# dt's 16 columns in a quarter of v: one step fewer in the mixer of a hybrid decoder layer, and five stretches of written order

## The chip, the cores and the metric

The kernel runs on one core of one Trainium2 chip. The metric is the time of one execution in microseconds (us), the median of the runs. Engines are named as the profile names them: PE is TensorE (matmuls; PEld its weight loads), DVE is VectorE, ACT is ScalarE, POOL is GpSimd, SP is SyncE, whose queue issues most of the loads.

## What is computed

One decoder layer over 512 tokens of width 1024: a SwiGLU FFN, a mixer, a second FFN, a gated embedding, and a last norm. The mixer is the part that the change is about:

```python
n = rmsnorm(h, mix_norm[i])
proj = n @ w_in[i]
u, v, z, xbc, dt_raw = jnp.split(proj, IN_SPLITS, axis=-1)
ya = chunked_spatial_gating(jax.nn.gelu(u, approximate=False), jax.nn.gelu(v, approximate=False), ...)
ya = rmsnorm(ya, gm_out_norm[i])
yb = mamba2_mixer(z, xbc, dt_raw, conv_w[i], conv_b[i], dt_bias[i], a_log[i], d_skip[i], ssm_norm[i])
h = h + jnp.concatenate([ya, yb], axis=-1) @ w_out[i]
```

Of `w_in`'s 4624 columns, u, v and z have 1024 each, xbc has 1536 (x 1024, B 256, C 256) and dt has 16, one for each head of the SSM. Inside `mamba2_mixer`, xbc goes through a causal convolution of width 4 and silu, and dt through a softplus with a bias; dt then scales x and, cumulatively summed, makes the decays. v is used after gelu and a layer norm over its 1024 columns.

## The kernel before

All matmuls keep near-float32 precision by splitting each operand into a high and a low part: `whi` is a copy of a weight tile rounded by ACT (the **cast**), `wlo` is what is left, taken on DVE (the **low**). A product is then three matmuls (`passes`, L219): hi x hi, hi x lo, lo x hi.

The work is a list of **steps**. A step has a load (SP's queue, 512 KB, 128x1024), a cast, a low, a product on PE, and work after the product. There are 2 steps of embedding, 98 of the first FFN, 37 of the mixer, 16 of the output projection, and then the second FFN. For the mixer the steps are, in order (L1177):

```python
"B0 B1 dt C0 C1 x0 v0 x1 x2 x3 v1 x4 x5 v2 x6 x7 z0 v3 z1 v4 z2 v5 z3 v6 z4 v7 z5 u0 z6 u1 z7 "
"u2 u3 u4 u5 u6 u7"
```

B, C, x, z and u are projections onto 128 columns for all 512 tokens: 24 matmuls of 512 columns. v is needed with tokens on the partitions, so a v step takes two of the eight 128-row pieces of the contraction and adds them into four PSUM banks, one for each 128 tokens, 512 columns of v wide: 24 matmuls of 512 columns. v0 to v3 make v's first half, v4 to v7 the second; gelu reads the four banks after v3 and after v7 (`v_kept`).

dt has a step of its own (`dt_step`, L1143): its 16 columns, twice, fill a 128-column tile so that one product of 16 matmuls gives the high and the low half. dt comes out with heads on the partitions; `dt_kept` copies it (L1262), four transposes on PE put tokens on the partitions (L1267), `dt_sum` adds the halves, applies the norm's row scale `rtok` and the bias, and `softplus` follows. `sums_of_adt`, `decays_of_sums`, `sums_by_row` and `rows_to_dram` make the decays from it.

B and C pass through `conv`: `begin` copies a product out of its bank, scaled by the norm's row scale (L1228), `end` does three operations of DVE for the taps (L1238), and a silu on ACT follows. The norm of the mixer's input itself is made while B0 and B1 run: sums of squares on PE (L288), a chain of small operations on DVE, a broadcast on PE (L325). The input x is split by ACT (L210) and DVE (L211), and B0 takes its last two pieces of x behind its other six.

Each engine runs its instructions in the order in which the program issues them. That order is set by `run`: for each step it issues product, cast (two steps ahead), low, the work after the step before, and so on, and each of these is a task with a name (load, product, cast, split for the low, after, rest, post, and the number of the step). The table `ENTRY` is an order written out by hand for the first stretch of the program: names of tasks, with a count of pieces where only a part of it is issued. What `ENTRY` does not name is issued in `run`'s own order behind it. Tiles come from rings of buffers: `whi`, `wlo` and `raw` have three each, so the cast of a step waits for the product of the third step before.

In the FFNs, a group makes gate and up products into banks named mm and a (L725), DVE and ACT turn them into g, which is split into `ghi` (ACT, L894) and `glo` (DVE, L896), and the down product (L235) goes into banks named sm, which DVE adds to h (L930). `whix` and `wlox` are the halves of the down weights.

Of the kernel before, what the change touches and what calls it, by code (L numbers as in the profile page):

```python
# [60 lines left out]
after13  # L61
# [16 lines left out]
HEADS = 16  # L78
HD = 64
# [20 lines left out]
def layer_kernel(ctx: ExitStack, tc: tile.TileContext, a: dict, out: bass.AP):  # L100
# [254 lines left out]
    class RowNorm(Norm):  # L355
# [52 lines left out]
    def run(steps, opened, order):  # L408
# [64 lines left out]
    class Parts:  # L473


        def __init__(self, tag="raw"):
            self.tag, self.n = tag, 1024

        def load(self, src, n=1024):
            self.n = n  # L480
# [5 lines left out]
            nc.sync.dma_start(self.raw[:, :n], src)  # L486
# [22 lines left out]
        def cast(self, x=""):  # L509
            self.take(x)  # L510
            nc.scalar.copy(self.hi[:, : self.n], self.raw[:, : self.n])  # L511

        def low(self):
            n = self.n
            nc.vector.tensor_tensor(  # L515
                self.lo[:, :n], self.raw[:, :n], self.hi[:, :n].bitcast(F32), ALU.subtract
            )
# [577 lines left out]
    w_in, w_v = a["w_in"], a["w_v"]  # L1095
# [30 lines left out]
    def dt_step():  # L1126

        w = Parts()
        got = {}

        def low():
            got["both"] = w.hi.rearrange("p (k m) -> p k m", k=ND)
            nc.vector.tensor_tensor(
                got["both"][:, :, HEADS : 2 * HEADS],
                w.raw.rearrange("p (k m) -> p k m", k=ND)[:, :, :HEADS],
                got["both"][:, :, :HEADS].bitcast(F32), ALU.subtract,
            )

        def product():
            got["ps"] = bank("mm", 3)  # L1140
            for k in range(ND):
                for i in range(2):
                    nc.tensor.matmul(  # L1143
                        got["ps"], got["both"][:, k, :], x[k][i], start=k + i == 0, stop=k + i == ND
                    )

        step = Step(product, lambda: w.load(w_in[0]), None, low, urgent=True)
        step.cast = w.cast
        step.got = got
        return step  # L1150

# [3 lines left out]
    def v_step(n):  # L1155

        half, u = divmod(n, 4)
        w = Parts()

        def product():  # L1160
            if u == 0:
                v_ps[:] = [four_ps(i) for i in range(NC)]
            for c in range(NC):
                for i in range(2):
# [5 lines left out]
        step = Step(product, lambda: w.load(w_v[half, u]), None, w.low, urgent=True)  # L1170
        step.cast = w.cast
        return step

    def chunk(t, c):
# [3 lines left out]
        "B0 B1 dt C0 C1 x0 v0 x1 x2 x3 v1 x4 x5 v2 x6 x7 z0 v3 z1 v4 z2 v5 z3 v6 z4 v7 z5 u0 z6 u1 z7 "  # L1178
        "u2 u3 u4 u5 u6 u7"
    ).split()  # L1180
    UNITS = {"B": 1, "C": 3, "x": 5, "z": 13, "u": 21}
    at = {name: n for n, name in enumerate(ORDER)}
    mix_steps = []
    for name in ORDER:
        kind, i = name[0], int(name[1]) if name != "dt" else 0
        if name == "dt":
            step = dt_step()
        elif kind == "v":
            step = v_step(i)
# [8 lines left out]
    got = {name: step.got for name, step in zip(ORDER, mix_steps) if name[0] != "v"}  # L1198
# [61 lines left out]
    def dt_kept():  # L1260
        mix["dt_raw"] = tmp()
        nc.vector.tensor_copy(mix["dt_raw"][: 2 * HEADS], got["dt"]["ps"][: 2 * HEADS])  # L1262

    def dt_by_token():
        mix["dt_ps"] = ring_ps()
        for c in range(NC):
            nc.tensor.transpose(  # L1267
                mix["dt_ps"][:, 2 * c * HEADS : 2 * (c + 1) * HEADS],
                mix["dt_raw"][: 2 * HEADS, c * P : (c + 1) * P], ident[: 2 * HEADS, : 2 * HEADS],
            )  # L1270

# [4 lines left out]
    def dt_sum():  # L1276

        parts = mix["dt_ps"][:, : 2 * NC * HEADS].rearrange("p (c i h) -> p i h c", c=NC, i=2)
        dtb = vec[:, _COL["dt_bias"] : _COL["dt_bias"] + HEADS]
        nc.vector.tensor_copy(hc(dt), parts[:, 0])  # L1280
        nc.vector.tensor_tensor(hc(dt), hc(dt), parts[:, 1], ALU.add)
        nc.vector.tensor_tensor(
            hc(dt), hc(dt), mix["rtok"].unsqueeze(1).to_broadcast([P, HEADS, NC]), ALU.mult
        )
        nc.vector.tensor_tensor(hc(dt), hc(dt), over_chunks(dtb), ALU.add)
# [302 lines left out]
    def v_kept(half):  # L1588
        for c in range(NC):
            t = sb("ya")  # L1590
            nc.scalar.activation(t, v_ps[c], AF.Gelu, scale=mix["rtok"][:, c : c + 1])
            v[c][half] = t
# [247 lines left out]
def _laid_out(i):  # L1840
# [39 lines left out]
    for n in ("ffn1", "ffn2"):  # L1880
# [10 lines left out]
    dt = np.zeros((D, P), w.dtype)  # L1891
    dt[:, :HEADS] = dt[:, HEADS : 2 * HEADS] = w[:, 4608:]

    order = np.concatenate([dt, w[:, 4096:4608], w[:, 3072:4096], w[:, 2048:3072], w[:, :1024]], axis=1)
    o["w_in"] = units(order)
    o["w_v"] = np.ascontiguousarray(
        w[:, 1024:2048].reshape(4, 2, P, 2, T).transpose(3, 0, 2, 1, 4).reshape(2, 4, P, 2 * T)
    )
# [32 lines left out]
```

## Time and profile before

| | |
|---|---|
| median of 3 runs | 1079.78 us (1078.62 to 1080.32) |
| the profiled execution | 1078.85 us, its span 1077.1 us |
| PE busy | 1065.2 us |
| DVE busy | 780.1 us |
| ACT busy | 514.8 us |
| POOL busy | 136.2 us |
| granted clock of PE | 0.998 |

The span is the time between the first and the last instruction of the profile; the execution's own time lies around it. The profile gives the records of each instruction: start, length, and for an idle stretch in front of it what released the engine. Matmuls overlap in a pipeline and their ends are modelled, so a row's length says less than the distance between two starts.

### The profile page before, as it was taken

How to read it: one execution, taken by the hardware profiler on the slowest of the kernel's cores; microseconds unless marked ns; L12 is line 12 of the kernel's file. 1: busy time of each engine (PE TensorE's matmuls, PEld its weight loads, DVE VectorE, ACT ScalarE, POOL GpSimd, SP SyncE). 2: the span in 40 equal slices, each digit the busy share in tenths (PEclk: the TensorE clock that was granted, in tenths of full speed). 3: DMA queues.
4: the chain of work that ended last, by engine and by line, in shares of the span. 5: the costliest groups of instructions: out<-in, count | busy, mean ns of one | idle time of the engine just before them, and what ended most of it. 6: DMA issues, size and time to landing. Idle time of an engine off the chain costs nothing.

```text
span 1077.1 us, 18907 instructions
## 1 busy us (share of the span) xinstructions
PE 1065.2 (99%) x7850; PEld 992.3 (92%) x7850; DVE 780.1 (72%) x1081; ACT 514.8 (48%) x711; POOL 136.2 (13%) x125
## 2 busy tenths in 40 slices
PE   9999999999999999999999999999999999999997
PEld 8999999999999888787888888999999999999996
DVE  7987676666666686766997756688766676677766
ACT  6744444343444455575754334354444434343554
POOL 0100000000001201043233000000000000000311
PEclk9999999999999999999999999999999999999999
DMA  9986776665523232444432223667756676633412
GB/s 343 303 226 193 191 192 180 174 184 156 134 60 127 90 98 81 146 131 135 131 105 79 98 98 117 202 162 204 212 142 172 182 195 178 179 115 111 144 41 79
DMA packets 50038, 163.91 MB, mean 152 GB/s; under 512 B 5664, under 2 KB 6176, under 8 KB 49952
## 3 DMA queue, kind: packets, MB, share of 16 engines
q1 hardware_dynamic: 40016, 129.09, 34.4%
q0 software_dynamic: 8640, 31.46, 16.4%
q10 hardware_dynamic: 1296, 2.16, 0.6%
q8 instruction: 61, 1.00, 0.4%
q14 instruction: 25, 0.20, 0.1%
HBM read 158.43 MB, written 4.26 MB: 151 GB/s over the span
## 4 chain that ended last, share of the span: by engine, by line
PE 90%; DVE 4%; DMA 2%; ACT 2%; issue 1%; SPq 0%; DVEq 0%; ACTq 0%
PE sm L235 24%; PE mm L725 20%; PE a L725 15%; PE mm L219 6%; PE sm L219 6%; PE mm L235 6%; PE a L219 5%; PE a L235 3%; PE sm L814 2%; DMA whix<-in_x_rows 1%; PE mm L814 1%; PE a L814 1%; DVE wlo L515 1%; DMA raw<-in_ffn_gu 1%; PE sm L288 1%
## 5 line engine op out<-in xcount | busy, mean ns | idle before, releaser
L511 ACT CAST whi<-raw 128x1024 fp32r<-128x1024 f32 x138 | 144.3, 1046 | 160.6 <-issue 61.0
L515 DVE TENSOR_TENSOR wlo<-raw,whi 128x1024 fp32r<-128x1024 f32 x137 | 172.0, 1255 | 62.4 <-ACT whi L511 60.8
L725 PE MATMUL mm<-xfb,whi 128*128 128x256 f32 x960 | 166.2, 276 | 0.0
L235 PE MATMUL sm<-ghi,wlox 128*128 128x256 f32 x592 | 150.9, 277 | 0.3 <-DVE wlox L515 0.3
L235 PE MATMUL sm<-glo,whix 128*128 128x256 f32 (+1 forms) x512 | 151.1, 295 | 0.0
L235 PE MATMUL sm<-ghi,whix 128*128 128x256 f32 (+1 forms) x512 | 150.3, 294 | 0.0
L725 PEld LDWEIGHTS mm<-xfb,whi 128*128 128x128 f32 x960 | 144.6, 188 | 0.0
L725 PE MATMUL mm<-xfb,wlo 128*128 128x256 f32 x480 | 132.5, 276 | 0.0
L235 PEld LDWEIGHTS sm<-ghi,wlox 128*128 128x128 f32 x592 | 111.1, 188 | 7.5 <-DVE wlox L515 0.7
L725 PE MATMUL a<-xfb,whi 128*128 128x256 f32 x640 | 111.0, 276 | 0.0
L725 PEld LDWEIGHTS a<-xfb,whi 128*128 128x128 f32 x640 | 96.4, 188 | 0.2 <-issue 0.2
L235 PEld LDWEIGHTS sm<-ghi,whix 128*128 128x128 f32 x512 | 96.1, 188 | 0.0
L235 PEld LDWEIGHTS sm<-glo,whix 128*128 128x128 f32 x512 | 96.1, 188 | 0.0
L725 PEld LDWEIGHTS mm<-xfb,wlo 128*128 128x128 f32 x480 | 90.1, 188 | 0.0
L725 PE MATMUL a<-xfb,wlo 128*128 128x256 f32 x320 | 88.5, 276 | 0.0
L515 DVE TENSOR_TENSOR wlox<-rawd,whix 128x1024 fp32r<-128x1024 f32 (+1 forms) x40 | 45.7, 1142 | 58.2 <-ACT whix L511 58.2
L515 DVE TENSOR_TENSOR wlo<-rawb,whi 128x1024 fp32r<-128x1024 f32 x52 | 63.6, 1223 | 18.8 <-ACT whi L511 18.8
L874 ACT ACTIVATE g<-g 128x512 f32<-128x512 f32 x40 | 25.3, 632 | 106.8 <-DVE g L872 106.8
L740 POOL DMA_DIRECT2D raw<-in_ffn_gu x20 | 17.3, 866 | 418.0 <-DVE h L930 195.4
L511 ACT CAST whi<-rawb 128x1024 fp32r<-128x1024 f32 x52 | 54.3, 1044 | 27.2 <-DVE rawb L735 17.8
L930 DVE SCALAR_TENSOR_TENSOR h<-sm,h 128x512 f32<-128x512 f32 x96 | 63.2, 684 | 3.3 <-PE sm L235 3.2
L219 PE MATMUL sm<-x,whi 128*128 128x512 f32 x208 | 65.5, 396 | 0.0
(403 smaller groups left out, 2490.3 us busy)
## 6 DMA issues: line engine op xcount, KB each, us to landing
raw<-in_ffn_gu SPq DMA_DIRECT2D x56, 512.0 KB, 6.2
rawd<-in_ffn_down SPq DMA_DIRECT2D x40, 512.0 KB, 4.2
rawb<-in_ffn_gu SPq DMA_DIRECT2D x32, 512.0 KB, 5.6
raw<-in_ffn_gu POOLq DMA_DIRECT2D x30, 512.0 KB, 5.3
raw<-in_w_in SPq DMA_DIRECT2D x29, 512.0 KB, 3.5
s<-in_ffn_gu SPq DMA_DIRECT2D x20, 512.0 KB, 7.1
s<-in_ffn_gu POOLq DMA_DIRECT2D x20, 512.0 KB, 8.4
raw<-in_w_out SPq DMA_DIRECT2D x16, 512.0 KB, 3.4
```

The source lines that it names most:

```text
L219: nc.tensor.matmul(ps, w, x, start=first and n == 0, stop=last and n == 2, skip_group_check=True)
L235: nc.tensor.matmul(ps[:, tok], wt[:, c], xt[:, tok], start=first and k == i == 0, stop=last and k == len(xs) - 1 and i == len(by_part) - 1 ...
L288: nc.tensor.matmul(ps[:, c : c + 1], part[:, c * P : (c + 1) * P], ones[:, 0:1], start=part is t, stop=part is not t or more is None,)
L511: nc.scalar.copy(self.hi[:, : self.n], self.raw[:, : self.n])
L515: nc.vector.tensor_tensor(self.lo[:, :n], self.raw[:, :n], self.hi[:, :n].bitcast(F32), ALU.subtract)
L725: nc.tensor.matmul(o, wt[:, c], xt, start=fresh and p == m == n == 0, stop=last and n == 2, skip_group_check=True,)
L740: nc.gpsimd.dma_start(w21.raw, self.src[0], accum_op=ALU.add)
L814: nc.tensor.matmul(by_half(ps)[:, s], (whi, whi, wlo)[n][:, c], t[:, s, n % 2], start=not lower and p == i == 0, stop=lower and p == len(s ...
L874: nc.scalar.activation(t, t, AF.Silu)
L930: nc.vector.scalar_tensor_tensor(h[d], ps[d], 0.5, h[d], ALU.mult, ALU.add)
```

## The change

dt's step is gone. Its 16 columns are put behind the first 256 columns of v, as a 272-column quarter. v's first half is now made in two quarters: A0 to A3 (two pieces of the contraction each, 272 columns, back to back behind C1) and W0 to W2 (three, three and two pieces, 256 columns). v's second half stays as it was, under the names v0 to v3. The order is now:

```python
"B0 B1 C0 C1 A0 A1 A2 A3 x0 x1 W0 x2 x3 x4 W1 x5 x6 W2 x7 z0 z1 v0 z2 v1 z3 v2 z4 v3 z5 u0 "
"z6 u1 z7 u2 u3 u4 u5 u6 u7"
```

dt then comes out with tokens on the partitions, in columns 256 to 271 of the four banks of A: the copy, the transposes, and the sum of halves go, and four operations of DVE of 16 columns each read the banks. gelu of v's first half is done in two parts, one behind A3 and one behind W2. An A step loads 656 columns of a tile, W0 and W1 768, W2 512, at column 112 and on.

`ENTRY` gets five further stretches of written order. A name with two dots in front, new as well, means that everything up to that task is issued in `run`'s own order, and so marks the distance between stretches.

```diff
-after13
+after13 ..after23 split26:1 after23:2 split26 after23 ..split101 after98:1 split101 after98
+after+98 load104 product100 cast102 after+98 after99 rest100 split102 load105 split102 load105
...
+cast108 after105 ..split130 split130 after128.3 split130 post127 post127.1 rest128 load133
...
+after131.1 after131.2 after131.3 split134 post131 ..product163 product163 split165:1 product163
+after162 split165 load170 product164 split166 after163 after163.1 after164:1 product165 after164
...
+after+166 split171:1 after+166 after167 split170 sums171 load175 product169 after168
...
+            if entry.startswith(".."):
+                for name, task in tasks.items():
+                    if name == entry[2:]:
+                        break
+                    for _ in task:
+                        pass
+                continue
...
-    def dt_step():
...
+    def v_step(kind, i):
+
+        per, width, apart, offset = {
+            "A": (2, DT_END, 384, DT_AT), "W": (3, HT, HT, DT_AT), "v": (2, T, T, 0),
+        }[kind]
+        ks = range(per * i, min(per * (i + 1), ND))
         w = Parts()
 
         def product():
-            if u == 0:
-                v_ps[:] = [four_ps(i) for i in range(NC)]
+            if i == 0:
+                v_ps[:] = [four_ps(c) for c in range(NC)]
             for c in range(NC):
-                for i in range(2):
-                    k = 2 * u + i
+                for k in ks:
                     xhi, xlo = (chunk(t, c) for t in x[k])
-                    cols = slice(i * T, (i + 1) * T)
-                    passes(v_ps[c], xhi, xlo, w.hi[:, cols], w.lo[:, cols], k == 0, k == ND - 1)
+                    n = offset + apart * (k - ks[0])
+                    cols = slice(n, n + width)
+                    passes(v_ps[c][:, :width], xhi, xlo, w.hi[:, cols], w.lo[:, cols], k == 0, k == ND - 1)
...
+    def dt_kept():
+
         dtb = vec[:, _COL["dt_bias"] : _COL["dt_bias"] + HEADS]
...
+        for c in range(NC):
+            nc.vector.scalar_tensor_tensor(
+                hc(dt)[:, :, c], v_ps[c][:, HT:DT_END], mix["rtok"][:, c : c + 1], dtb, ALU.mult, ALU.add
+            )
...
-    first(3, dt_kept)
-    on_pe(4, dt_by_token)
-    first(5, dt_sum)
-    post(6, softplus)
-    on_pe(8, sums_of_adt)
-    first(9, decays_of_sums)
-    on_pe(9, sums_by_row)
-    first(10, rows_to_dram)
+    n = at["A3"]
+    first(n + 1, dt_kept)
+    post(n + 1, softplus)
+    on_pe(n + 3, sums_of_adt)
+    first(n + 4, decays_of_sums)
+    on_pe(n + 4, sums_by_row)
+    first(n + 5, rows_to_dram)
...
-    first(at["v3"] + 1, lambda: v_kept(0))
-    first(at["v3"] + 2, lambda: v_moments(0))
-    n = at["v7"]
-    first(n + 1, lambda: v_kept(1))
+    first(at["A3"] + 1, lambda: v_kept(0, halves[0]))
+    first(at["W2"] + 1, lambda: v_kept(0, halves[1]))
+    first(at["W2"] + 2, lambda: v_moments(0))
+    n = at["v3"]
+    first(n + 1, lambda: v_kept(1, whole[0]))
```

Here DT_AT is 112, HT 256, T 512 and DT_END 272. How the rows move on DVE is shown at three places. The line numbers of the changed kernel are some 15 to 26 higher.

DVE in the first FFN, at the group that reads its down weights at 94 us: `glo` is the low of the group's g, `wlox` the low of the down weights. Before, and with the change:

```order
L883 TENSOR_TENSOR g_1095<-g_1095,a_146_901 128x512
L896 TENSOR_TENSOR glo_1219<-g_1095,ghi_1218 128x1024
L515 TENSOR_TENSOR wlox_1223<-rawd_1065,whix_1222 128x1024
L735 TENSOR_TENSOR rawb_995<-rawb_995,s_163_1030 128x1024
L515 TENSOR_TENSOR wlo_1256<-rawb_995,whi_1255 128x1024
```

```order
L909 TENSOR_TENSOR g_1095<-g_1095,a_146_901 128x512
L541 TENSOR_TENSOR wlox_1218<-rawd_1065,whix_1217 128x1024
L922 TENSOR_TENSOR glo_1222<-g_1095,ghi_1221 128x1024
L761 TENSOR_TENSOR rawb_995<-rawb_995,s_163_1030 128x1024
L541 TENSOR_TENSOR wlo_1256<-rawb_995,whi_1255 128x1024
```

The low of the down weights now stands ahead of the low of g; the casts on ACT have changed places in the same way.

DVE at the end of the first FFN and the start of the mixer: h are the adds of the last down products, x the low parts of the mixer's input, wlo_4157 is the low of B1, whi_4197 dt's, and in the changed kernel wlo_4204 C0's. Before, and with the change:

```order
L515 TENSOR_TENSOR wlo_4157<-raw_3973,whi_4156 128x1024
L930 SCALAR_TENSOR_TENSOR h_97<-sm_4038,h_97 128x512
L930 SCALAR_TENSOR_TENSOR h_101<-sm_4061,h_101 128x512
L211 SCALAR_TENSOR_TENSOR x_4169<-h_97,vec_70,x_4168 128x512
L211 SCALAR_TENSOR_TENSOR x_4173<-h_101,vec_70,x_4172 128x512
L1133 TENSOR_TENSOR whi_4197<-raw_4036,whi_4197 128x8x16
L930 SCALAR_TENSOR_TENSOR h_98<-sm_4105,h_98 128x512
L930 SCALAR_TENSOR_TENSOR h_102<-sm_4128,h_102 128x512
L211 SCALAR_TENSOR_TENSOR x_4210<-h_98,vec_70,x_4209 128x512
L211 SCALAR_TENSOR_TENSOR x_4214<-h_102,vec_70,x_4213 128x512
L515 TENSOR_TENSOR wlo_4251<-raw_4103,whi_4250 128x1024
```

```order
L956 SCALAR_TENSOR_TENSOR h_97<-sm_4038,h_97 128x512
L541 TENSOR_TENSOR wlo_4157<-raw_3973,whi_4156 128x1024
L956 SCALAR_TENSOR_TENSOR h_101<-sm_4061,h_101 128x512
L229 SCALAR_TENSOR_TENSOR x_4169<-h_97,vec_70,x_4168 128x512
L229 SCALAR_TENSOR_TENSOR x_4173<-h_101,vec_70,x_4172 128x512
L956 SCALAR_TENSOR_TENSOR h_98<-sm_4105,h_98 128x512
L956 SCALAR_TENSOR_TENSOR h_102<-sm_4128,h_102 128x512
L229 SCALAR_TENSOR_TENSOR x_4209<-h_98,vec_70,x_4208 128x512
L229 SCALAR_TENSOR_TENSOR x_4213<-h_102,vec_70,x_4212 128x512
L541 TENSOR_TENSOR wlo_4204<-raw_4036,whi_4203 128x1024
L541 TENSOR_TENSOR wlo_4251<-raw_4103,whi_4250 128x1024
```

One add of h has gone ahead of B1's low; dt's subtraction is gone, and the last adds and x's last low parts stand ahead of C0's low.

DVE beside C1 and the A steps, with the change: the lows of 656 columns are those of A1, A2 and A3, the two of 1024 behind them x0's and x1's; convin 4353, 4396, 4401 and 4447 are B0's, B1's, C0's and C1's copies out of their banks.

```order
L541 TENSOR_TENSOR wlo_4349<-raw_4223,whi_4348 128x656
L1240 SCALAR_TENSOR_TENSOR ya_4356<-convin_4353,vec_70,ya_4356 128x512 x3
L1229 MEMSET convin_4396 128x3
L1230 TENSOR_TENSOR convin_4396<-mm_4225,rall_4351 128x512
L1229 MEMSET convin_4401 128x3
L1230 TENSOR_TENSOR convin_4401<-sm_4267,rall_4351 128x512
L541 TENSOR_TENSOR wlo_4393<-raw_4265,whi_4392 128x656
L1240 SCALAR_TENSOR_TENSOR ya_4399<-convin_4396,vec_70,ya_4399 128x512 x3
L1240 SCALAR_TENSOR_TENSOR ya_4404<-convin_4401,vec_70,ya_4404 128x512 x3
L1229 MEMSET convin_4447 128x3
L1230 TENSOR_TENSOR convin_4447<-sm_4323,rall_4351 128x512
L541 TENSOR_TENSOR wlo_4440<-raw_4321,whi_4439 128x656
```

Where three lows of A now stand between the convolutions, the kernel before had those of x0 and v0 and dt's copy.

More of the change, by code (lines that the diff above doesn't have):

```diff
@@ L78 @@
 HEADS = 16
+DT_AT = 112
+DT_END = HT + HEADS
 HD = 64
@@ L476, in __init__, with load @@
         def __init__(self, tag="raw"):
-            self.tag, self.n = tag, 1024
-        def load(self, src, n=1024):
-            self.n = n
+            self.tag, self.n, self.at = tag, 1024, 0
+        def load(self, src, n=1024, at=0):
+            self.n, self.at = n, at
             tag = self.tag
@@ L485, in load @@
             self.raw = sb(tag, (P, 1024))
-            nc.sync.dma_start(self.raw[:, :n], src)
+            nc.sync.dma_start(self.raw[:, at : at + n], src)
         def take(self, x=""):
@@ L510, in cast @@
             self.take(x)
-            nc.scalar.copy(self.hi[:, : self.n], self.raw[:, : self.n])
+            c = slice(self.at, self.at + self.n)
+            nc.scalar.copy(self.hi[:, c], self.raw[:, c])
         def low(self):
-            n = self.n
+            c = slice(self.at, self.at + self.n)
             nc.vector.tensor_tensor(
-                self.lo[:, :n], self.raw[:, :n], self.hi[:, :n].bitcast(F32), ALU.subtract
+                self.lo[:, c], self.raw[:, c], self.hi[:, c].bitcast(F32), ALU.subtract
             )
@@ L1094, in layer_kernel @@
     x = x_mix
[L1095 removed]
+    w_in = a["w_in"]
     small = lambda tag: sb(tag, (P, HEADS * NC))
@@ L1124, in projection @@
         return step
-    def dt_step():
[L1128 to L1141, printed above, removed]
-                for i in range(2):
[L1143 to L1150, printed above, removed]
     v = [[None, None] for _ in range(NC)]
     v_ps = []
-    def v_step(n):
-        half, u = divmod(n, 4)
+    def v_step(kind, i):
[3 more added lines that the diff above has]
+        ks = range(per * i, min(per * (i + 1), ND))
         w = Parts()
         def product():
-            if u == 0:
-                v_ps[:] = [four_ps(i) for i in range(NC)]
+            if i == 0:
+                v_ps[:] = [four_ps(c) for c in range(NC)]
             for c in range(NC):
-                for i in range(2):
-                    k = 2 * u + i
+                for k in ks:
                     xhi, xlo = (chunk(t, c) for t in x[k])
-                    cols = slice(i * T, (i + 1) * T)
-                    passes(v_ps[c], xhi, xlo, w.hi[:, cols], w.lo[:, cols], k == 0, k == ND - 1)
-        step = Step(product, lambda: w.load(w_v[half, u]), None, w.low, urgent=True)
+                    n = offset + apart * (k - ks[0])
+                    cols = slice(n, n + width)
+                    passes(v_ps[c][:, :width], xhi, xlo, w.hi[:, cols], w.lo[:, cols], k == 0, k == ND - 1)
+        n = apart * (len(ks) - 1) + width
+        step = Step(product, lambda: w.load(a["w_" + kind][i, :, :n], n, offset), None, w.low, urgent=True)
         step.cast = w.cast
@@ L1184, in layer_kernel @@
     for name in ORDER:
[L1185 to L1189, printed above, removed]
+        kind, i = name[0], int(name[1])
+        if kind in "AWv":
+            step = v_step(kind, i)
         else:
@@ L1197, in layer_kernel @@
         mix_steps.append(step)
-    got = {name: step.got for name, step in zip(ORDER, mix_steps) if name[0] != "v"}
+    got = {name: step.got for name, step in zip(ORDER, mix_steps) if name[0] not in "AWv"}
     def first(n, fn):
@@ L1258, in over_chunks @@
         return t.unsqueeze(2).to_broadcast([P, HEADS, NC])
[L1260 to L1270, printed above, removed]
     sp = [small(f"sp{i}") for i in range(4)]
@@ L1586, in layer_kernel, with v_kept @@
     v_stats = []
-    def v_kept(half):
+    def v_kept(half, cols):
         for c in range(NC):
-            t = sb("ya")
-            nc.scalar.activation(t, v_ps[c], AF.Gelu, scale=mix["rtok"][:, c : c + 1])
-            v[c][half] = t
+            if cols.start == 0:
+                v[c][half] = sb("ya")
+            nc.scalar.activation(
+                v[c][half][:, cols], v_ps[c][:, : cols.stop - cols.start], AF.Gelu,
+                scale=mix["rtok"][:, c : c + 1],
+            )
     def v_moments(half):
```

39 lines of the change are left out of this document (22 added, 17 removed).

## The prediction

> **What bounds the kernel now.** I read the page first, then the chain of waits, then the timeline of TensorE (PE) around the places the change touches.
>
> ```profile
> span 1077.1 us, 18907 instructions
> PE 1065.2 (99%) x7850; PEld 992.3 (92%) x7850; DVE 780.1 (72%) x1081; ACT 514.8 (48%) x711; POOL 136.2 (13%) x125
> PE 90%; DVE 4%; DMA 2%; ACT 2%; issue 1%; SPq 0%; DVEq 0%; ACTq 0%
> ```
>
> PE is busy for 99% of the span and makes 90% of the chain. So time comes only from less PE work, or from one of the few places where PE stands still. Work taken from VectorE (DVE), ScalarE (ACT) or DMA counts only where PE waits for it.
>
> **What a matmul costs.** Ends of matmuls are modelled, so I use the distance from one start to the next, which the chain shows as a length over a count. The first lines are of the step dt and its transposes, the next two together are one step of v (24 matmuls of 512 columns), and the last is a run of 256-column matmuls in an FFN.
>
> ```profile
> 363.40 0.79 PE sm L288 x8
> 364.18 3.78 PE mm L1143 x16
> ...
> 379.44 0.36 PE sm L1267 x4
> 379.80 5.71 PE a L219 x24
> ...
> 409.39 4.09 PE mm L219 x18
> 413.49 1.36 PE a L219 x6
> ...
> 722.93 2.15 PE a L725 x19
> ```
>
> A v step takes 4.09 + 1.36 = 5.45 us, 227 ns for a matmul of 512 columns. 2.15 / 19 = 113 ns is the price at 256. Half the columns cost half the time, 0.443 ns a column. The eight one-column matmuls at L288 take 0.10 us each, so there is a floor of about 100 ns under any matmul with a weight load of its own; 256 and 272 columns both lie above it.
>
> **The dt edit, part by part.**
>
> Removed from PE: dt's 16 matmuls, 3.78 us. The four transposes, 0.36 us, and what they disturb: the step behind them took 5.71 us for 24 matmuls, against 5.45, so 0.26 us more. Together 4.40 us.
>
> Added to PE: v's first half was 4 steps x 24 = 96 matmuls of 512 columns, 21.8 us. It becomes 96 of 272 (the steps A) and 96 of 256 (the steps W): 96 x 16 = 1536 column times more, 1536 x 0.443 ns = 0.68 us. The trace has no 272-column matmul. From below it costs no less than one of 256 (113 ns, growth nothing), from above no more than one of 512 (227 ns, growth 96 x 114 ns = 10.9 us). I take 120.5 ns, because 256 and 512 lie on one line through zero. PE's work: -4.40 + 0.68 = -3.72 us.
>
> The Trainium skill, page "TensorE: Matmul & The Clock Gate", section "Back-to-back issue gap", speaks against this: it gives a sustained 81 ns a matmul at 128 columns and 131 ns at 512, so halves cost far more than half. Interpolating, my estimate from that page is 98 ns at 256 and 100 ns at 272: v's first half would go from 12.6 to 19.0 us, and the edit would lose some 4 us after dt's 16 x 131 ns are taken off. This trace disagrees (227 and 113 ns).
>
> On the other engines, dt's copy, four small operations and a small subtraction leave DVE, and four 16-column operations that read v's banks come. Lows are one per step: the four of v and dt's become seven, of 656 (A), 768 and 512 (W) columns instead of 1024. The gelu of v's first half is cut in two parts, which needs one more pass over four banks and one more table load on ACT.
>
> ```profile
> L515 DVE TENSOR_TENSOR wlo<-raw,whi 128x1024 fp32r<-128x1024 f32 x17 | 21.3, 1251 | 2.0 <-ACT whi L511 2.0
> L1238 DVE SCALAR_TENSOR_TENSOR ya<-convin,vec,ya 128x512 f32<-128x512 f32 x12 | 8.9, 749 | 0.3
> L1228 DVE TENSOR_TENSOR convin<-sm,rall 128x512 f32<-128x512 f32 x8 | 5.5, 690 | 8.3 <-PE sm L219 8.2
> L1244 ACT ACT_TABLE_LOAD x4 | 5.1, 1283 | 0.1
> ```
>
> A low of 656 columns costs between 656/1024 of 1.25 us, 0.80, and 1.25 us; I take 0.85. All of this is at zero in the sum: the cover is PE's own stream, 5.45 us and more for a step, while DVE works 72% and ACT 48% of the time. The table load is 1.28 us in an ACT that has half of its time free. SP issues seven loads where five were, of 336, 384 or 256 KB instead of 512, and less in all; steps behind dt move up one place in SP's queue, and C0's load takes the place that dt's had. That cover is thinnest in one place. A0 to A3 stand back to back and last 24 x 120.5 ns = 2.9 us each, half of a v step. From C1's start, when the row scale r has just left PE, A3 begins after C1 and three A steps, 5.45 + 3 x 2.9 = 14.2 us. Ahead of the end of A3's low DVE has to do nine convolution steps (9 x 0.75), four copies out of banks (4 x 0.69) and three lows (3 x 0.85), 12.1 us, some of it behind ACT's work on the same tiles. That leaves about 2 us less those waits; I count on one. If that fails, each microsecond late is a microsecond of PE. The bounds are 0 and 2.5 us (three convolution steps and copies more than counted); I take 0.3.
>
> **The written order: stalls of PE.** I searched the starts of PE for gaps beyond the price by columns. Five lie where rows move; a sixth stays.
>
> ```profile
> 94.53 0.40 PE L235 MATMUL sm<-glo,whix 128*128 128x512 f32 x1
> 95.23 0.39 PE L235 MATMUL sm<-ghi,wlox 128*128 128x256 f32 x1 [0.30 <-DVE wlox L515]
> ...
> 348.29 0.28 PE L235 MATMUL sm<-ghi,wlo 128*128 128x256 f32 x1
> 348.85 0.47 PE L235 MATMUL sm<-ghi,whi 128*128 128x512 f32 x1 [0.29 <-DVE h L930]
> ...
> 356.51 0.39 PE L219 MATMUL mm<-x,whi 128*128 128x512 f32 x1
> 357.20 0.50 PE L219 MATMUL mm<-x,whi 128*128 128x512 f32 x1 [0.30 <-DVE x L211]
> ...
> 727.55 0.28 PE L235 MATMUL sm<-ghi,wlox 128*128 128x256 f32 x1
> 727.87 0.47 PE L725 MATMUL a<-xfb,whi 128*128 128x256 f32 x2
> ...
> 739.21 0.39 PE L725 MATMUL a<-xfb,whi 128*128 128x256 f32 x2
> 739.63 0.39 PE L725 MATMUL a<-xfb,wlo 128*128 128x256 f32 x1
> ...
> 541.86 0.44 PE L1471 MATMUL sm<-u,yb 128*64 128x128 f32 x4 [0.68 <-DVE u L1461]
> ```
>
> Start to start less the price by columns: 0.70 - 0.23 = 0.47; 0.56 - 0.11 = 0.45; 0.69 - 0.23 = 0.46; 0.32 - 0.11 = 0.21; 0.42 - 0.23 = 0.19. Three of the matmuls behind a stall also show a longer record (0.47 and 0.50 against 0.39), about 0.1 us each. Sum 1.78 + 0.28 = 2.06 us. What each waited for on DVE and ACT:
>
> ```profile
> 91.73 1.05 ACT L894 CAST ghi<-g 128x1024 fp32r<-128x1024 f32 x1 [3.87 <-DVE g L883]
> 92.82 1.23 DVE L896 TENSOR_TENSOR glo<-g,ghi 128x1024 fp32r<-128x1024 f32 x1 [1.12 <-ACT ghi L894]
> 93.96 1.22 DVE L515 TENSOR_TENSOR wlox<-rawd,whix 128x1024 fp32r<-128x1024 f32 x1
> ...
> 346.88 1.22 DVE L515 TENSOR_TENSOR wlo<-raw,whi 128x1024 fp32r<-128x1024 f32 x1 [3.20 <-ACT whi L511]
> 348.02 1.28 DVE L930 SCALAR_TENSOR_TENSOR h<-sm,h 128x512 f32<-128x512 f32 x2
> ...
> 352.96 0.29 DVE L1133 TENSOR_TENSOR whi<-raw,whi 128x128 fp32r<-128x128 f32 x1 [1.12 <-ACT whi L511]
> 353.17 1.28 DVE L930 SCALAR_TENSOR_TENSOR h<-sm,h 128x512 f32<-128x512 f32 x2
> 354.64 2.50 DVE L211 SCALAR_TENSOR_TENSOR x<-h,vec,x 128x512 fp32r<-128x512 f32 x2 [0.20 <-ACT x L210]
> ...
> 725.91 1.22 DVE L515 TENSOR_TENSOR wlo<-raw,whi 128x1024 fp32r<-128x1024 f32 x1
> 727.04 0.68 DVE L867 TENSOR_TENSOR g<-a,p 128x512 f32<-128x512 f32 x1
> 735.97 1.22 DVE L735 TENSOR_TENSOR raw<-raw,s 128x1024 f32<-128x1024 f32 x1
> 738.35 1.23 DVE L515 TENSOR_TENSOR wlo<-raw,whi 128x1024 fp32r<-128x1024 f32 x1 [1.17 <-ACT whi L511]
> ```
>
> At 94 us wlox stood behind glo, which waited for ghi, while ACT had been idle for 3.87 us; now whix is cast ahead of ghi and wlox goes first, some 1.2 us earlier against 0.47 needed. What waits behind it now, glo, is read a whole group later. At 348 us DVE stood 3.20 us in front of wlo, with the add that frees PE's bank queued behind it; now the first add goes ahead. At 356 us both adds and the last two lows of x stood behind dt's small subtraction and its cast; both lows of w now follow them, and DVE's idle 1.12 us ahead of 352.96 shows the room. At 727 us the operation that empties bank a goes ahead of a low. At 739 us the sum raw + s stands further up, but its start may be bound by when s lands: a gain between 0 and 0.19. At 541 us the same DVE work still precedes u, so I leave that stall. I count all five as gone, 2.06 us; the bounds are 0, if each wait is replaced by an equal one, and 2.06.
>
> **The sum.** -3.72 - 2.06 + 0.30 = -5.48 us. The profiled execution took 1078.85 us (span 1077.1 and 1.75 around it), which gives 1073.4. The median of the runs, 1079.78, lies 0.9 above it, and the same sum gives 1074.3 from there. I forecast the middle, **1073.9 us**.
>
> **The rivals.**
>
> (1) The order only moves the stalls. PE sits at 99%, so what it saves brings it sooner to the next producer: DVE had 1.12 and 3.20 us of room ahead of some stalls, but in the second FFN hardly any between 725 and 728. With 2.06 given back, -3.4 us: 1076 us.
>
> (2) The A block starves PE. Four short steps need four lows and casts in 11.6 us, beside the convolutions of B and C. For it speaks the thin cover of about 1 us; against it, that DVE's 12.1 us fit into 14.2. At its bound of 2.5 us, with the stalls gone: -3.3 us, 1076.1; with rival 1 too, -1.2 us, about 1078.1 and no measurable change.
>
> (3) The slower side: 272 columns are not charged by the column. The place is the 96 matmuls of A, the price anything up to 227 ns each. It decides from 120.5 + 5480/96 = 178 ns: above that the kernel is slower than before. If past 256 a second pass of 256 is charged, growth is 10.9 in place of 0.68, so -5.48 + 10.2 = +4.7 us, about 1084. Against it: 512 costs exactly twice 256, and weight loads (100 ns) fit under both; for it: no row lies between 256 and 512. A milder form is that every half of a cut matmul costs more than half, 272 and 256 columns alike: with 145 ns for each of the 192 it is 192 x 28 = 5.4 us more, just the gain; 19 matmuls of 256 columns in 2.15 us speak against it. The Trainium skill's sustained figures, named above, would end on this side, with a loss of some 2 us once the stalls are counted as gone.
>
> **Chances.** Forecast 66%, its own range 1072.2 to 1075.4; rival 1 17%; rival 2 8%, half of it without measurable change; rival 3 4%; 5% for a gain or loss that I have not seen, such as a new wait in the z steps, where z0 and z1 now stand together and ACT has two steps of z without a v between. Range: from 1071.9 (runs at the fast end, and the restarts fewer) to 1077.0, which takes in rival 1 and rival 2 alone. About 0.2%, 2.2 us, is what a measurement of this kernel can tell from no change: faster means below 1077.6. The forecast, rival 1, half of rival 2 and some of the unseen give 0.88 faster; 0.07 the same; 0.05 slower.
>
> **What would show it.** In the changed profile an A quarter of 24 matmuls should take 2.9 us and a W step of 36 should take 4.1; no PE gap of 0.4 us at the five places, shifted earlier; the one at u still there with about 1 us; no wait of PE on wlo within A0 to A3; PE's busy time some 3.5 us less. A steps of 3.5 us or more would prove the third rival; PE idle on wlo in them, the second; gaps at new places in the same stretches, the first.

## The result

The changed kernel takes 1073.45 us (median of 4 runs, 1072.92 to 1073.80), the one before 1079.46 us in the same comparison. The medians lie 6.0 us apart. The ratio of the runs is 0.9948, with a 95% interval of 0.9935 to 0.9960: 5.6 us less, between 4.3 and 7.0. The forecast was 1073.9.

The page of the changed kernel, the lines that answer to those of before:

```profile
span 1072.1 us, 19079 instructions
PE 1060.2 (99%) x7926; PEld 993.7 (93%) x7926; DVE 781.4 (73%) x1082; ACT 514.2 (48%) x716; POOL 135.5 (13%) x125
PE 93%; DVE 4%; ACT 2%; DMA 1%; issue 0%; SPq 0%; DVEq 0%; ACTq 0%
```

PE's busy time went down by 5.0 us and so did the span (1077.1 to 1072.1). DVE has 1.3 us more work, ACT 0.6 less, and neither is seen in the time. The chain of waits around the A steps and the first two W steps shows what took dt's place (lengths over counts):

```profile
362.05 0.79 PE sm L306 x8
362.83 5.59 PE sm L237 x24
...
374.32 2.22 PE mm L237 x18
376.54 0.74 PE a L237 x6
...
398.65 3.07 PE mm L237 x27
401.72 1.02 PE a L237 x9
...
420.57 3.18 PE mm L237 x27
423.75 1.06 PE a L237 x9
```

C0 follows the row sums at once, where dt's 3.78 us stood. An A step takes 2.22 + 0.74 = 2.96 us, 123 ns a matmul. W0 takes 4.09 us, 114 ns a matmul, and W1 4.24, 118 ns. So v's first half is 4 x 2.96 + 4.09 + 4.24 + 2.83 (W2, 24 matmuls at W1's price) = 23.0 us against 21.8: it grew by 1.2 us, not by 0.68.

What PE still waits for:

```profile
PE sm L202 <- DVE tmp L199: 1.7, 1, 1.7
PE sm L1060 <- ACT ghi L1047: 1.4, 1, 1.4
PE sm L1800 <- DVE tmp L1751: 0.8, 1, 0.8
PE sm L1457 <- DVE u L1447: 0.7, 1, 0.7
PE sm L1551 <- DVE convin L221: 0.4, 1, 0.4
```

The waits on wlox, on h and on x that stood at 94, 348 and 356 us are gone, and the starts of PE's matmuls show no gap at the two places of the second FFN either. The first three lines are the program's start and end; the second moves between 0 and 1.4 us from one execution to the next, as the others below show. The fourth is the stall at u that I left in place (L1471 in the kernel before). The last is new. PE's timeline and DVE's show it:

```profile
545.04 0.40 PE L1551 MATMUL sm<-convin,onesr 128*128 128x512 f32 x1
545.87 0.50 PE L1551 MATMUL sm<-convin,onesr 128*128 128x512 f32 x1 [0.44 <-DVE convin L221]
```

```profile
541.04 0.41 DVE L1591 BATCH_NORM_AGGREGATE vstat<-bnst 128x2 f32<-128x12 f32 x4
541.49 0.76 DVE L262 TENSOR_SCALAR nv<-vstat 128x4 f32<-128x4 f32 x1
...
542.49 1.14 DVE L265 TENSOR_TENSOR nt<-ny 128x4 f32<-128x4 f32 x1
...
545.13 0.69 DVE L221 TENSOR_TENSOR convin<-xs,convin 128x512 fp32r<-128x512 f32 x1
```

The written order has moved the chain that makes v's norm factor (BATCH_NORM_AGGREGATE and the small operations behind it, 4.1 us with two of them stretched) ahead of convin's low, which PE's sums need. 0.83 us from start to start, less 0.23, is a gap of 0.60 us, and the matmul behind it is 0.1 us longer (a restart). In the kernel before, convin's low came first, and the chain began 3.6 us behind it, at 549.14 us:

```profile
545.53 0.68 DVE L203 TENSOR_TENSOR convin<-xs,convin 128x512 fp32r<-128x512 f32 x1
```

To see where the time went I cut the profiled executions at the first one-column matmul of each group of row sums, which stand at the same place of the program in all kernels. The kernels below are introduced in the next section.

| stretch of the program, us | before | changed | dt edit alone | order alone | factor late | low behind u |
|---|---|---|---|---|---|---|
| start, first FFN, to the mixer's first sums | 363.23 | 361.88 | 364.14 | 361.83 | 362.48 | 361.35 |
| mixer, to the sums of y's first group | 152.25 | 149.09 | 149.08 | 152.23 | 149.09 | 149.09 |
| to the sums of y's second group | 55.48 | 56.21 | 55.51 | 55.53 | 55.49 | 54.40 |
| to the last matmul | 499.05 | 497.90 | 498.88 | 498.08 | 497.92 | 498.08 |

Two differences in this table do not come from a row that was moved. The first row holds the program's start, and that moves from one execution to the next: the eleven profiles of the changed kernel and of those variants of it that keep its order there lie between 361.1 and 362.5 us. How far two executions have drifted apart before the first moved row is seen at the first matmul of the down product in which the stall at 94 us lies, here of the kernel before and of the changed one:

```profile
94.31 0.39 PE L235 MATMUL sm<-ghi,whix 128*128 128x512 f32 x1
```

```profile
94.58 0.39 PE L253 MATMUL sm<-ghi,whix 128*128 128x512 f32 x1
```

The changed kernel was 0.27 us late there, and the one with the order alone (94.69) 0.38. From there on to the first sums the changed kernel gains 1.62 us, not the 1.35 of the table. The last row holds 0.17 us from a run of 46 matmuls at about 1025 us, at 118 ns each in the kernel before and 113 in the changed one; the dt edit alone has this too, without the written order.

### The profile page after: what moved, and what is told of

It is laid out like the page before. It is cut to its first block, busy times and chain, and to the rows that moved or that the text cites. A ratio compares the mean times of both kernels' runs of the same rounds, so it can differ in the third digit from the quotient of the medians.

```text
span 1072.1 us, 19079 instructions
## 1 busy us (share of the span) xinstructions
PE 1060.2 (99%) x7926; PEld 993.7 (93%) x7926; DVE 781.4 (73%) x1082; ACT 514.2 (48%) x716; POOL 135.5 (13%) x125
## 4 chain that ended last, share of the span: by engine, by line
PE 93%; DVE 4%; ACT 2%; DMA 1%; issue 0%; SPq 0%; DVEq 0%; ACTq 0%
PE sm L253 24%; PE mm L751 20%; PE a L751 15%; PE mm L237 6%; PE sm L237 6%; PE mm L253 6%; PE a L237 4%; PE a L253 3%; PE sm L840 2%; PE mm L840 1%; PE a L840 1%; DMA g<-in_p 1%; PE sm L1393 1%; PE sm L1633 1%; PE sm L306 0%; DVE tmp L1745 0%
## 5 line engine op out<-in xcount | busy, mean ns | idle before, releaser
L541 DVE TENSOR_TENSOR wlo<-raw,whi 128x1024 fp32r<-128x1024 f32 (+1 forms) x140 | 172.7, 1234 | 60.5 <-ACT whi L537 58.8
L537 ACT CAST whi<-raw 128x1024 fp32r<-128x1024 f32 (+1 forms) x140 | 144.3, 1032 | 150.3 <-issue 56.5
L237 PE MATMUL sm<-x,whi 128*128 128x512 f32 x224 | 71.0, 398 | 0.0
```

The costliest lines, as they stand in the source:

```text
L237: nc.tensor.matmul(ps, w, x, start=first and n == 0, stop=last and n == 2, skip_group_check=True)
L537: nc.scalar.copy(self.hi[:, c], self.raw[:, c])
L541: nc.vector.tensor_tensor(self.lo[:, c], self.raw[:, c], self.hi[:, c].bitcast(F32), ALU.subtract)
```

## The experiments

**The dt edit alone.** The changed kernel without the five stretches:

```diff
-after13 ..after23 split26:1 after23:2 split26 after23 ..split101 after98:1 split101 after98
...
-after+166 split171:1 after+166 after167 split170 sums171 load175 product169 after168
+after13
```

> The changed kernel without the five stretches of written order: the dt edit alone. By my sum the stretches are worth 2.06 us, so this kernel is 3.4 us faster than the one before (1076 us against 1079.5), and the stalls of PE at 94, 348 and 356 us, and at 727 and 739 us of the old time, are there again. If the profile's longer A and W steps are right (23.6 us for v's first half against 21.8, where I had counted 0.68 more), only 2.6 us are left, 1076.9. If the order is worth nothing, it is as fast as the changed kernel, 1073.5.

Measured: 1076.26 us against 1079.20, ratio 0.9974 (0.9965 to 0.9983): 2.8 us less, between 1.8 and 3.8, which takes in both 3.4 and 2.6. PE's waits and the place at 356 us:

```profile
PE mm L221 <- DVE x L213: 1.1, 1, 1.1
...
PE sm L237 <- DVE wlox L525: 0.5, 1, 0.5
PE sm L237 <- DVE h L940: 0.3, 1, 0.3
```

```profile
353.08 1.23 DVE L525 TENSOR_TENSOR wlo<-raw,whi 128x1024 fp32r<-128x1024 f32 x1 [1.05 <-ACT whi L521]
...
355.70 2.33 DVE L213 SCALAR_TENSOR_TENSOR x<-h,vec,x 128x512 fp32r<-128x512 f32 x2 [0.19 <-ACT x L212]
```

```profile
355.96 0.39 PE L221 MATMUL mm<-x,whi 128*128 128x512 f32 x1
357.42 0.50 PE L221 MATMUL mm<-x,whi 128*128 128x512 f32 x1 [1.08 <-DVE x L213]
```

The two stalls of the second FFN are too short for this list, but from the second group of y on to 739 us PE runs in step with the kernel before, so they are there too. The one at x has grown: 1.46 us from start to start, 1.23 of them gap, where it was 0.46. C0's low of 1.23 us has taken the place of dt's of 0.29 ahead of the adds and of x. So the dt edit makes a stall of its own, which the written order then takes away together with the old one. The new wait on convin is not in this kernel, and the mixer's middle has the whole gain of the changed kernel, 3.17 us.

**The order alone.** The kernel before, with the stretch in the first FFN, the first lines of the one at the mixer's start, and the one in the second FFN (step numbers two lower, since v's quarters are missing):

```diff
-after13
+after13 ..after23 split26:1 after23:2 split26 after23 ..split101 after98:1 split101 after98
+after+98 load104 product100 cast102 after+98 after99 rest100 split102
+..product161 product161 split163:1 product161
...
```

> The kernel before with its dt step, and with three of the stretches: the one in the first FFN, the first lines of the one at the mixer's start, the one in the second FFN. The two stretches inside the mixer are left out. By my sum all five stalls go, 2.06 us: 1077.4 us. If the order only moves the stalls, 1079.5.

Measured: 1076.45 us against 1079.20, ratio 0.9975 (0.9966 to 0.9985): 2.7 us less, between 1.6 and 3.7. In the waits of this kernel nothing is left between the start and u:

```profile
PE sm L191 <- DVE tmp L188: 1.7, 1, 1.7
PE sm L1824 <- DVE tmp L1775: 0.8, 1, 0.8
PE sm L1485 <- DVE u L1475: 0.7, 1, 0.7
PE sm L1048 <- ACT ghi L1035: 0.3, 1, 0.3
```

The stalls go and no other takes their place: the first rival falls for these stretches. The table gives 1.40 us in its first row and 0.97 in its last. With the 0.38 us by which this execution came late to the first stall, the first is 1.79 us, and the two are 2.75, where I counted 1.58 and 0.48. So the profile agrees with the 2.7 of the runs. In the second FFN more goes than the two gaps. Of the kernel before and of the changed one, a run of 256-column matmuls from the chain of waits, behind the place of the first of them:

```profile
734.00 2.59 PE mm L725 x22
```

```profile
726.76 5.44 PE mm L751 x48
```

Before, PE ran at 2.59 / 22 = 118 ns a matmul from the stall at 727.6 us on until the next at 739 us, 82 matmuls; in the changed kernel it runs at 113. Those 82 x 4.4 ns are another 0.36 us. In the kernel with the dt edit alone, which has the stall, 72 matmuls from 725.8 us on run at 118 as well; with the order alone they run at 113. That the stall caused the slower pace is not shown, only that the two go together in these four kernels. The other 0.3 us are spread over the five places, whose restarts I had priced at three.

**The factor of v in its old place.** The entry `post131.1` (and a second `after131` behind it) taken out of the changed kernel's order, so that the chain of the norm factor is issued behind convin's low, the copy of u, a low of w and the offsets:

```diff
-split133 post130 rest131 rest131.1 load136 product132 cast134 after131 post131.1 after131
+split133 post130 rest131 rest131.1 load136 product132 cast134 after131
```

> The changed kernel with one entry of its order less: the chain that makes v's norm factor (from the aggregation of the batch norm on) goes back behind the low of the gate's mask weights, the copy of u, the low of w and the offsets. If that chain is what holds convin back and makes PE wait 0.6 us at 545 us, that gap goes, with its 0.1 us restart: 0.7 us less than the changed kernel, 1072.8. If the norm of v then comes too late for the spatial product, a wait of up to 0.7 us appears after 550 us and the time stays at 1073.5.

Measured: 1072.85 us against 1079.20, ratio 0.9943 (0.9931 to 0.9956). The two matmuls of the sums follow each other again, in one row of the timeline,

```profile
545.63 0.63 PE L1551 MATMUL sm<-convin,onesr 128*128 128x512 f32 x2
```

and the third stretch of the table is 0.72 us shorter than in the changed kernel, with no new wait behind it. Measured once more, on one chip with the changed kernel, it was:

> The kernel with the factor of v late once more, on the same chip as the changed kernel: 0.6 us less than it if the removed gap is time, the same if the gap was slack.

1072.48 us (1072.38 to 1073.01), and the changed kernel

> The changed kernel once more, as the mark for the two others of this call: 1073.4 us, with the gap of 0.6 us at 545 us, the A steps at 123.3 ns a matmul, the first W step at 113.3 and the other two at 117.7.

1073.37 us (1073.05 to 1073.82), five runs each, which do not overlap: 0.9 us between the medians, 0.7 of which the third stretch of their profiles shows. The gap was time.

**What a column costs.** The A steps with 384 columns instead of 272, the further ones of zero weights:

```diff
-            "A": (2, DT_END, 384, DT_AT), "W": (3, HT, HT, DT_AT), "v": (2, T, T, 0),
+            "A": (2, 384, 384, DT_AT), "W": (3, HT, HT, DT_AT), "v": (2, T, T, 0),
```

> The A steps with 384 columns instead of 272, the further 112 columns of zero weights. By the column: 384 x 0.443 = 170 ns a matmul, 4.08 us a step; 96 x 112 x 0.443 = 4.8 us more in all, 1078.2. If a fixed surcharge of 3 to 4.5 ns lies on every matmul of a step (272 columns took 123.4 ns instead of 120.5), 173 to 175 ns. If past 256 a second pass of 256 were charged, 227 ns, but then 272 would have shown it.

Measured: 1079.07 us in one run, 5.6 more than the changed kernel, where 4.8 was expected. An A step:

```profile
374.54 3.18 PE mm L237 x18
377.72 1.06 PE a L237 x6
```

4.24 us, 176.7 ns a matmul, where 170 was expected by the column. The slope from 272 to 384 columns is (176.7 - 123.3) / 112 = 0.48 ns a column, against 0.443. The third rival falls: there is no step past 256 columns, but there is a surcharge of 3 to 7 ns above the line through 256 and 512, and it is not a fixed one.

**The tile's column.** A and W steps read their tiles from column 112 on. The same with column 0, and with 128:

```diff
-DT_AT = 112
+DT_AT = 0
```

> The changed kernel with the A and W tiles at column 0 instead of 112. If the offset of 448 bytes makes the matmuls of 272 columns take 123.4 ns instead of 120.5 and two thirds of those of 256 columns 117.7 instead of 113.3, they come back to the line: A steps 2.89 us instead of 2.96, W steps of 36 at 4.08 instead of 4.23, 0.5 us in all. If the surcharge belongs to a mode that PE falls into on its own, the pitches stay as they are.

> The same with column 128, a multiple of 512 bytes: again the line if the offset is the cause, 123.4 and 117.7 ns if it is not.

Measured in one run each: 1074.12 and 1075.00 us. The chain of waits of the kernel with column 0, three quarters of an A step and of W0, and of that with column 128, three quarters of an A step:

```profile
373.92 2.25 PE mm L237 x18
...
398.43 3.23 PE mm L237 x27
```

```profile
374.74 2.25 PE mm L237 x18
```

Both expectations are missed, and the opposite is true: at 0 and 128 the matmuls are slower than at 112, 125.5 ns at 272 columns and 120 at 256, alike for both. The column matters, and 112 is the better one. A last kernel gave each tile its own column:

```diff
+        offset = {"A0": 16, "A1": 64, "A2": 100, "A3": 240, "W0": 64, "W1": 240, "W2": 16}.get(f"{kind}{i}", offset)
```

> The changed kernel with another column for each tile: A0 at 16, A1 at 64, A2 at 100, A3 at 240, W0 at 64, W1 at 240, W2 at 16. At column 112 the A steps took 123.3 ns a matmul, at 0 and 128 125.4. If the pitch depends on the tile's column, the four A steps differ, and one with the worth of 112 is found among 16 and 240 (odd multiples of 16 columns), one with that of 128 at 64; if 0 and 128 were slow for another reason, all four are alike. W0 was 113.3 at 112 and 120 at 0 and 128.

Measured: 1073.99 us in one run. Three quarters of each of the four A steps, in order:

```profile
373.96 2.28 PE mm L237 x18
...
377.00 2.28 PE mm L237 x18
...
380.04 2.24 PE mm L237 x18
...
383.35 2.23 PE mm L237 x18
```

A0 (16) and A1 (64) took 126.6 ns a matmul, A2 (100) 124.4, A3 (240) 123.3. So the pace follows the column, and 240 is worth what 112 is: they are 128 columns apart, as 0 and 128 are. Of 16 and 240, one of which I expected to be like 112, it is 240; 16 is as slow as 64. W0 at 64 took 120 ns, W1 at 240 117.7, W2 at 16 117.7; at 112 W0 took 113.4 and both others 117.7, so for 256 columns the tile's column is not all of it. No column tried brings 272 columns to the 120.5 ns of the line.

**The cover of the A block.** A3's low done four times:

```diff
+        def low():
+            for _ in range(4 if kind == "A" and i == 3 else 1):
+                w.low()
...
```

> The changed kernel with A3's low done four times: 3 x 0.83 = 2.5 us more on DVE ahead of A3. In the profile of the changed kernel the low is ready 1.2 us before A3 starts, so PE should now wait 1.3 us in A3 (the first matmul on the low part is the third), and x0's low, which had 3 us, should still be in time: 1.2 to 1.3 us more in all. If DVE's slack is larger than I read it, no wait; if the wait carries on into x0, over 2 us.

Measured: 1074.99 us in one run. PE in A3, and DVE:

```profile
383.00 0.37 PE L237 MATMUL mm<-whi,x 128*128 128x272 f32 x1
384.50 0.39 PE L237 MATMUL mm<-wlo,x 128*128 128x272 f32 x1 [1.13 <-DVE wlo L541]
```

```profile
380.99 4.59 DVE L541 TENSOR_TENSOR wlo<-raw,whi 128x656 fp32r<-128x656 f32 x5
```

The row of DVE holds A3's four lows and behind them x0's, of 1024 columns (4 x 0.83 + 1.22). The gap is 1.50 - 0.12 = 1.38 us, and x0 does not wait: the mixer's stretch is 150.50 us, 1.41 more than in the changed kernel. With 2.5 us added, 1.1 to 1.2 were free. The second rival's place is real, and in the changed kernel it is covered with a microsecond to spare.

**u ahead of the norm steps.** On top of the factor late, the last norm steps of y's first group go behind the product u of z6:

```diff
-split132 post129 post129.1 load135 product131 cast133 after130 after130.1 after130.2 after130.3
-split133 post130 rest131 rest131.1 load136 product132 cast134 after131
+split132 post129.1 load135 product131 cast133 after130 after130.1 after130.2 after130.3
+split133 post129 post130 rest131 rest131.1 load136 product132 cast134 after131
```

> The kernel with the factor of v late, and one entry more moved: the last two norm steps of the first group of y, and their split, go behind the product of the decays u of z6 on DVE. The stall of PE that I left in place (about 0.9 us at 537 us, waiting for u) should go, because u then runs 4 us earlier: 1071.9 us. If what makes u late is POOL sharing the way to the tiles and not the order, u stays late by half, 1072.4; if the steps moved back are needed sooner than I think, a new wait appears and the time stays at 1072.9.

Measured: 1073.81 us (1073.51 to 1076.06), ratio 0.9958 (0.9944 to 0.9971), about a microsecond slower than with the factor late alone; the third stretch is 56.84 us, 1.35 more. The stall at 537 us is gone and a longer one stands at 549 us. From its cause to PE:

```profile
541.12 0.64 POOL L1543 TENSOR_SCALAR_AFFINE_SELECT xs<-xs 128x512 f32<-128x512 f32 x1 [0.25 <-DMA xs<-in_gm_w]
```

```profile
542.44 1.12 DVE L221 TENSOR_TENSOR convin<-xs,convin 128x512 fp32r<-128x512 f32 x1 [2.66 <-ACT convin L220]
```

```profile
549.19 0.39 PE L237 MATMUL mm<-x,wlo 128*128 128x512 f32 x1
551.29 0.95 PE L1457 MATMUL sm<-u,yb 128*64 128x128 f32 x6 [1.71 <-DVE u L1447]
```

The second load of the gate's weights lands late, POOL's mask, ACT's cast and DVE's low pass that on, DVE stands idle for 2.66 us, and everything behind convin, down to the next u, is late. The load goes into the ring xs, whose buffers those norm steps free, and the trace shows the link: SP waits 7.9 us with this load for DVE's split of yb, the last of the steps that went back, and issues it at 537.42 us, as the first of the two splits ends. With the factor late alone it waits for the same split and issues the load 4.4 us earlier, counted from the sums of y's first group.

**A low behind u.** On top of the factor late, only a low of w for z7 goes behind u, and the norm steps stay:

```diff
-split132 post129 post129.1 load135 product131 cast133 after130 after130.1 after130.2 after130.3
-split133 post130 rest131 rest131.1 load136 product132 cast134 after131
+post129 post129.1 load135 product131 cast133 after130 after130.1 after130.2 after130.3
+split132 split133 post130 rest131 rest131.1 load136 product132 cast134 after131
```

> The kernel with the factor of v late, and one entry more moved: a low of w for z7, 1.67 us on DVE, goes behind the product of the decays u of z6, and nothing else. z7 needs that low some 3 us later than u is needed, so the stall of PE at u (0.92 us) should go, without delaying the norm steps that freed a buffer too late in the kernel with u first: 0.9 us less than the kernel with the factor late. If u is then only half as early because POOL stretches the steps before it, 0.4 us less; if the low becomes late for z7, nothing is won.

Measured: 1071.85 us (1071.33 to 1072.11) against 1079.31, ratio 0.9931 (0.9919 to 0.9944). The third stretch of the table is 1.09 us shorter than with the factor late. DVE's u is done before PE comes to it, and the list of PE's waits holds only the start and the end of the program:

```profile
533.01 2.38 DVE L1447 TENSOR_TENSOR u<-u,ya 128x512 f32<-128x512 f32 x2
```

```profile
535.70 1.09 PE L1457 MATMUL sm<-u,yb 128*64 128x128 f32 x16
```

```profile
PE sm L202 <- DVE tmp L199: 1.7, 1, 1.7
PE sm L1800 <- DVE tmp L1751: 0.8, 1, 0.8
```

The two u still take 2.38 us, as in the kernel before, where others of their kind take 1.28; what helped is that they start 1.3 us earlier, counted from the sums of y's first group. Beside it on the same chip, the kernel with the factor late took 1072.48 us and the changed one 1073.37, so it is 0.6 and 1.5 us faster than these by the medians, with no overlap of the runs (0.9 was expected, and the third stretch shows 1.1), and 7.5 faster than the kernel before.

## Why the prediction was right, point by point

**What bounds the kernel.** Right: the span fell with PE's work and PE's gaps, and 1.3 us more of DVE cost nothing. One sign was misread: PE's busy time was to fall by some 3.5 us and fell by 5.0. It counts part of a stall as busy (of the gap of 0.47 us at 94 us the list of waits has 0.30), so the stalls that went are in it too.

**The dt edit.** -4.40 was right in its kind: the mixer's middle lost 3.16 us in the changed kernel and 3.17 with the dt edit alone, against -3.72 forecast. The term that was mis-sized is v's growth, 0.68 us: it is 1.2. Half of the rest is the A steps (123.3 ns for 120.5), half W1 and W2 (117.7 for 113.4). I drew a line through the 256-column matmuls of an FFN and the 512-column ones of v; the short matmuls of v, from tiles at another column, do not lie on it.

**The rule set against it.** By my estimate from the Trainium skill's sustained figures, page "TensorE: Matmul & The Clock Gate", section "Back-to-back issue gap", 256 columns cost some three quarters of 512. Here they cost 113 to 120 ns against 227, so halving a matmul costs at most 6% more; no row of this case has 512 columns at the 131 ns of those figures.

**The cover of the A block.** I counted 12.1 us of DVE against 14.2, took one microsecond as spare and put 0.3 into the sum. The spare time measured 1.1 to 1.2 us, and the 0.3 was not needed.

**The order.** All five stalls went, as forecast. Their worth was 2.06 us by the gaps; alone the order brings 2.75 us by the profile and 2.7 (1.6 to 3.7) by the runs, more than the 2.06 that I had called the bound. Two things were missed. In the second FFN the slower pace between the two gaps went too, 0.36 us. And I costed C0's low at its new place at nothing: without the order it would have made the stall at x 0.8 us longer. So the two parts do lean on each other at this one place. That their gains alone, 2.8 and 2.7, still add up to 5.5, about the whole, is chance: the 0.8 that the order takes away again in the changed kernel is offset by the 0.7 of the new wait on convin, which neither part alone has.

**What I did not see.** The wait on convin, 0.7 us. I gave the stretches inside the mixer no term in the sum, with 5% for something unseen "such as a new wait in the z steps"; what I should have done is to look at what the moved chain passes: it is 4 us long on DVE and went ahead of a low that PE was to need a few microseconds later.

**The sum.** By the profile: -4.40 + 1.2 for the dt edit, -2.6 for the order, +0.7 for convin, 0 for the A block, +0.3 for the late start of this execution and -0.2 for the pace at 1025 us: -5.0, which is what the span lost. The forecast was -5.48. The growth of v (0.5 short) and convin (0.7) were against me, the order (0.5) and the A block (0.3) for me. That the forecast of 1073.9 missed by only 0.4 is in part luck: its errors cancelled in part, and it stood between the profiled execution and the median.

**The rivals.** That the order only moves the stalls: false for the three stretches outside the z steps, true in kind for the one within that was tried by itself, where the stall at convin is the price. That the A block starves PE: false, by 1.1 us. That 272 columns are not charged by the column: true by 3 ns, where 57 would have been needed to turn the sign.

## What to carry to other kernels

On a kernel whose PE is busy for 99%, list PE's gaps from start to start and name for each the instruction that stands ahead of the late producer on its engine; moving one instruction was worth about its gap here, and the price is to be looked for at what the moved piece passes: the chain of small operations that cost convin, the freed buffer that cost u. Before moving a step away, ask what will stand in its place on every engine; the full low in place of dt's small one nearly tripled a stall. Where short matmuls are many, measure their pace at the place where they will run and not at another.

## What the runs showed that I had not expected

The pace of short matmuls depends on the column at which the moving tile begins. At 272 columns it was 123.3 ns at columns 112 and 240, 124.4 at 100, 125.5 at 0 and 128, and 126.6 at 16 and 64; at 256 columns 113.4, 117.7 or 120 ns. Whole steps run at one pace. At 512 columns it was 227 ns throughout, with the granted clock at 1.00 in all these stretches. A pace of 118 in place of 113 also stood between two stalls of an FFN whose tiles had not moved. What decides between the paces beyond the column stays open: W0 and W1 read the same columns at 113.4 and 117.7 ns, in every profile with column 112, and of the steps with 384 columns, all at 112, the first three took 176.7 ns and A3 174.0.
